# Four local edits to a four-sublayer encoder kernel: value products in banks of their own, another order of units in the down projections, the bias lines as rounded products, and turned blocks placed in two steps

## The chip, the cores and the metric

The kernel runs on one core of a Trainium2 chip. A core has a matrix engine (TensorE, PE in the profile, with its weight loads shown apart as PEld), a vector engine (VectorE, DVE), an engine for activations (ScalarE, ACT), one for general work (GpSimd, POOL) and one that here only issues transfers (SyncE, SP). PE writes into PSUM, eight banks of 128 partitions by 512 f32 numbers; everything else lies in SBUF or in device memory. The metric is the device time of one execution in microseconds.

## The reference

The input is 256 positions of 2048 numbers. Two layers run one after the other, each a token mixer and a gated MLP, all with a root-mean-square norm ahead and a residual sum behind:

```python
def reference(x, ...):
    h = x
    for i in range(2):
        hn = rms_norm(h, mix_norm[i])
        if i % 2 == 0:
            h = h + mixer_a(hn, ...)      # 16 query heads, 4 key heads, rotary positions, dense softmax
        else:
            h = h + mixer_b(hn, ...)      # 3 groups of 8 heads, dilations 1, 4, 16, windowed softmax
        h = h + conv_ffn(rms_norm(h, ffn_norm[i]), ...)
    return rms_norm(h, final_norm)

def conv_ffn(h, w_up, conv_w, conv_b, w_down):
    u = conv_width_3(h @ w_up, conv_w) + conv_b
    gate, val = split(u, 2)               # 5632 columns each
    return (silu(gate) * val) @ w_down

# in mixer_b, for each group g:
    bias = rel_bias_g[t5_bucket(rel * dilation)]          # 32 buckets x 8 heads
    logits = q k^T * scale + bias, -1e30 outside the window
    o = softmax(logits) @ v               # the value product
# and the groups are weighted by their softmax denominators
```

All of it is f32, and the weights (430 MB) pass through the core once.

## The kernel before

**Rounded halves.** The f32 products are made of three products of a rounded f32 type (F32R): a number is a high part, rounded by ACT, and a low part, which DVE gets by subtraction. A weight block is a `raw` of 512 KB (128 x 1024 numbers). `split_raw` turns it into `wh` (line 128, ACT) and `wl` (line 129, DVE), and `feed` makes 12 matmuls of 512 columns with it: high by high (line 153), low by high (154), high by low (155). Six `raw` buffers are loaded ahead by SP's queue. The split parts have a ring of three buffers, of four in the down projections.

**What sets the order.** The program is written as one long row of `feed` calls. Everything else (evacuation of a finished accumulator, rotary turn, softmax, convolution, residual sums) is a Python generator in the list `pending`, and `step()` runs the next piece of the first of them behind each half `feed`, so that its instructions stand between matmuls in the program. A scheduler then puts each engine's instructions in order by priority. `split_raw` gets 45 places of priority ahead of where it is written, so that splits pass other work on ACT and DVE. Within one engine the order is then fixed.

**PSUM.** Banks 0 to 3 hold the accumulators of projections, two at a time. Banks 4 to 7 are handed out in turn by `ps_tile()` for all that is small: transposes, scores, value products, bias lines.

**Value products (mixer B).** Group g has four heads in each half `hf` of the heads. `v_gen` runs by a plan, one entry a step: probabilities are scaled and turned (`turn`), put in place (`place`), rounded (`low`), multiplied (`value`). `value(i)` makes six matmuls of 256 columns for g = 0 (lines 307 to 309) into half a bank, then `split` reads it: `ah` on ACT (line 290), `al` on DVE (line 291). Heads 0 and 1 share a bank, and so do heads 2 and 3:

```python
                    def value(i):
                        j = i % 2
                        if j == 0:
                            parts["o"] = ps_tile()
```

**Down projections.** Two blocks of 512 output columns are made together in `project_pair`. Of the k-blocks, two (`SKG`) are multiplied by a scheme of seven products of sums in place of eight ("P" units of 6 matmuls; the products 1, 5, 6, 7 go into banks `M1`, `M5`, `M6`, `M7`, the others straight into an accumulator), and the others as usual ("c" units of 12 matmuls, into `C11`, `C21` or `C12`, `C22`). A P unit may need a sum of two raw blocks, which DVE makes (line 242). `weave` lays the units in a row. In the pair (0, 1) four c units stand first, then P and c units in turn until the c units run out; in the pair (2, 3) one stands first. When a block's last unit is done, its accumulator is added to the residual `h` by DVE (line 408). `combine` makes the sums of the seven products (lines 625 to 637). `late_at` is the first unit of the last k-block: before it, all pending work is drained.

**Bias lines (mixer B's bias, made during the first MLP).** `bias_lines` is a side generator that `step()` advances when fewer than two others are pending. It loads a one-hot table `oh` of 128 x 1024 (which bucket a distance falls in) and the 32 x 24 table of biases `rb`, spreads the biases over 32 columns each (`lh`, line 902, DVE) and makes `lh^T oh` in f32: six matmuls (line 908), two of 512 and four of 256 columns. DVE copies each out (`lnt`, line 911) and POOL's queue stores it to device memory (line 915), from where mixer B reads it much later.

**Turned blocks.** A transposition of 128 x 1024 numbers is made by DVE in 32 x 32 blocks (`turn_blocks`, line 335), and 16 copies put the blocks where they belong (`place_blocks`): 4 by POOL (line 345), 12 by ACT (line 347). `turned` issues all 16 in one step; `late_transpose` and `heads_T_dve` then wait two steps before they use the result.

Of the kernel before, what the change touches and what calls it, by code (L numbers as in the profile page):

```python
# [7 lines left out]
F32 = mybir.dt.float32  # L8
F32R = mybir.dt.float32r
AF = mybir.ActivationFunctionType  # L10
ALU = mybir.AluOpType
AX = mybir.AxisListType

P = 128
# [19 lines left out]
def tile_encoder(ctx: ExitStack, tc: tile.TileContext, x, xT, w_a, w_ao, q_gain, k_gain, w_b, w_bo,  # L34
                 rel_bias, gains, w_up, conv, w_down, final_norm, rope, ident_c, onehot, out):
    nc = tc.nc
# [23 lines left out]
    def nm(s):  # L60
        uid[0] += 1
        return f"{s}_{uid[0]}"
# [6 lines left out]
    def ps_tile():  # L69
        bank_at[1] = (bank_at[1] + 1) % 4  # L70
        return bank(4 + bank_at[1], "ps")
# [221 lines left out]
    def split_scaled(hi, lo, src, sc):  # L293
        nc.scalar.activation(hi, src, AF.Copy, scale=sc)
        if lo is None:
            return
        nc.vector.scalar_tensor_tensor(lo, src, sc, hi.bitcast(F32), ALU.mult, ALU.subtract)
# [18 lines left out]
    def new_hT(kt):  # L316
        t = hpool.tile([P, 2 * NT], F32R, tag=f"x{kt}", name=nm("xh"))
        return t[:, :NT], t[:, NT:], t
# [13 lines left out]
    def turn_blocks(s, pool, tag):  # L332
        t = pool.tile([P, 2, 512], F32, tag=tag, name=nm("tT"))
        for m in range(2):
            nc.vector.transpose(t[:, m], s[:, m])
        return t

    def place_blocks(o, t, place, part=range(16)):
        tv = t.rearrange("p m (j q c) -> p j m q c", j=4, q=4)
        for i in part:  # L340
            a, b = i // 4, (i // 4 + i) % 4
            dst = o[32 * b:32 * b + 32, :, :, 32 * a:32 * a + 32]
            src = tv[32 * a:32 * a + 32, :, :, b]
            if place[b] == "p":
                nc.gpsimd.tensor_copy(dst, src)  # L345
            elif place[b] == "a":
                nc.scalar.activation(dst, src, AF.Copy)  # L347
            else:
                nc.vector.tensor_copy(dst, src)

    def turned(o, s, pool, tag):
        t = turn_blocks(s, pool, tag)
        yield
        place_blocks(o.rearrange("p j (m t) -> p j m t", m=2), t, "paaa")

    def late_transpose(hT, n, g, pool, tags):
        def put(kt, src):
            hT[kt] = new_hT(kt)
            split_scaled(*hT[kt][:2], src, gain[:, g, kt:kt + 1])

        yield
        if n < 3:
            yield
            o = pool.tile([P, 4, NT], F32, tag=tags[1], name=nm("tM"))
            yield from turned(o, h[:, :, n * 512:(n + 1) * 512], pool, tags[0])
            yield
            yield
            for j in range(4):
                if j == 2:
                    yield  # L370
                put(4 * n + j, o[:, j, :])
            return
        yield
        for kp in range(2):
            if kp:
                yield
            t = ps_tile()
            for j in range(2):
                kt = 4 * n + 2 * kp + j
                for m in range(2):  # L380
                    nc.tensor.transpose(t[:, j * NT + m * P:j * NT + (m + 1) * P],
                                        h[:, m, kt * P:(kt + 1) * P], ident)
            for j in range(2):
                put(4 * n + 2 * kp + j, t[:, j * NT:(j + 1) * NT])
# [31 lines left out]
    def ffn(l, hT, ss_in, g_next, last, side=None):  # L416
        with tc.tile_pool(name=nm("wpool"), bufs=1) as wp, tc.tile_pool(name=nm("fpool"), bufs=1) as fp:
# [3 lines left out]
            part = small.tile([P, 2], F32, tag="part", name=nm("part"), bufs=1)  # L421
# [97 lines left out]
            for hf, (p0, p1) in enumerate(HALVES):  # L519
# [89 lines left out]
                ps = [("P", k, p) for k in SKG[hf] for p in ORDER]  # L609
                def weave(lead):  # L610
                    c, units = list(cs), []
                    units += [c.pop(0) for _ in range(lead)]
                    for u in ps:
                        units += [u] + [c.pop(0) for _ in range(min(1, len(c)))]
                    return units + c

                hl_ring.insert(0, (wp, 9))
# [90 lines left out]
    def heads_T_dve(o, s, pool, tag):  # L708
        hi, lo = o
        dst = hi if lo is None else s.rearrange("p m c -> p (m c)").rearrange("p (j t) -> p j t", j=4)  # L710
        yield from turned(dst, s, pool, tag)
        yield
        yield
        if lo is not None:
            split(hi, lo, dst)
# [175 lines left out]

    def bias_lines(wp, lp):
        if True:
            oh = wp.tile([P, 1024], F32, tag="wh9", name="oh")
            nc.gpsimd.dma_start(oh, onehot)
            rb = lp.tile([P, 32], F32, name="rb")[:, :24]
            nc.gpsimd.memset(rb, 0.0)
            nc.gpsimd.memset(rb[32:33, :], -1e30)
            nc.gpsimd.dma_start(rb[:32, :], rel_bias)
            lh = wp.tile([P, 24, 32], F32, tag="wl9", name="lh")  # L900
            lnt = lp.tile([P, 2, 512], F32, tag="tT", name="lnt")
            nc.vector.tensor_copy(lh, rb[:, :, None].to_broadcast([P, 24, 32]))
            for b in range(6):
                for _ in range(2):
                    yield
                c0, w = ((0, 512), (512, 256), (768, 256))[b // 2]
                t = ps_tile()
                nc.tensor.matmul(t[:, :w], lh[:, 4 * b:4 * b + 4, :].rearrange("p a r -> p (a r)"),
                                 oh[:, c0:c0 + w], start=True, stop=True)
                ln = lnt[:, b % 2]  # L910
                nc.vector.tensor_copy(ln[:, :w], t[:, :w])
                dst = scr0[4 * b:4 * b + 4] if b < 2 else scr1[4 * (b - 2):4 * (b - 2) + 4]
                for i in range(4):
                    yield
                    nc.gpsimd.dma_start(dst[:, 32 * i:32 * i + 32, :], ln[:, :w])

    def mixer_b(hT, ss_in):
        with tc.tile_pool(name="bpool", bufs=1) as bp:
# [26 lines left out]
            for hf in range(2):  # L945
# [56 lines left out]
                def v_gen(g, accs, hf=hf, probs=probs, e=e):  # L1002
# [31 lines left out]
                        split(*parts[i], src)  # L1034

                    def value(i):
                        j = i % 2
                        if j == 0:
                            parts["o"] = ps_tile()
                        o, pT = parts["o"], parts.pop(i)  # L1040
                        for kt in range(2):
                            vs = (allp, kt, slice(i * P, (i + 1) * P))
                            if g == 0:
                                mm3(o[:, j * NT:(j + 1) * NT], v, pT, vs,
                                    (allp, slice(kt * NT, (kt + 1) * NT)), kt == 0, kt == 1)
                            else:
                                mm3(o[:, j * NT + kt * P:j * NT + (kt + 1) * P], v, pT, vs,
                                    (allp, slice(kt * P, (kt + 1) * P)), True, True)
                        sl = (2 * g + hf) * 4 + i
                        slots[sl] = new_slot(sl)  # L1050
                        split(*slots[sl], o[:, j * NT:(j + 1) * NT])
# [110 lines left out]
```

## Time and profile before

| | |
|---|---|
| time, median of 3 runs | 2263.91 us (2262.77 to 2263.95) |
| the profiled execution | 2264.28 us, its span 2262.5 us |
| PE busy | 2241.2 us, 99% of the span |
| DVE busy | 1671.3 us, 74% |
| ACT busy | 1535.6 us, 68% |
| POOL busy | 299.2 us, 13% |
| matmuls of 512 columns in F32R | 9527, one every 0.227 us where nothing waits |
| moved | 437 MB, 193 GB/s over the span |

The profile page gives busy time of each engine, the span in 40 slices, the DMA queues, the chain of work that ended last, and groups of instructions by line. In a row of the timeline stand the start, the time taken, the engine, the line, the operation, what is written and read, the shape, and in brackets the idle time ahead with what ended it. Matmuls overlap in the pipeline, so the time of one in a row (0.39 us) is longer than the step from one start to the next (0.23 us); what is lost is read from the starts. The profiled execution is 0.37 us over the median of the runs, and 1.8 us of it lie outside its span.

### The profile page before, as it was taken

What the parts mean: (1) busy time and instruction counts of PE and PEld (TensorE: products, weight loads), DVE (VectorE), ACT (ScalarE), POOL (GpSimd) and SP (SyncE); (2) the same over time, 40 slices, a digit from 0 to 9 for tenths busy, and PEclk for the clock granted to TensorE, in tenths of its full rate; (3) what the DMA queues carried; (4) which work ended last, traced back from release to release, by engine and by line L of the source; (5) the groups of instructions that cost most, each with busy time, mean ns of one, the idle gap of its engine ahead of it and who ended that gap; (6) DMA issues with size and microseconds to landing.
All of it is one profiled execution on the core that took longest, in us unless ns stands there. A gap on an engine that the chain in (4) does not pass through costs nothing.

```text
span 2262.5 us, 28925 instructions
## 1 busy us (share of the span) xinstructions
PE 2241.2 (99%) x10093; PEld 1853.5 (82%) x10093; DVE 1671.3 (74%) x2267; ACT 1535.6 (68%) x2400; POOL 299.2 (13%) x436
## 2 busy tenths in 40 slices
PE   9999999999999999999999999999999999999998
PEld 7788888888888888888878887888888888888886
DVE  6776678888878788856575557465888788688895
ACT  6665777777547777767775777565777754577763
POOL 2211102210001010121130103000101100001101
PEclk9999999999999999999999999999999999999999
DMA  8444667765665655666655564655665656556654
GB/s 297 158 149 149 191 198 217 227 198 192 207 203 187 199 190 188 204 223 203 190 173 180 177 194 160 186 195 188 197 191 192 204 188 212 188 193 193 226 191 136
DMA packets 126452, 437.43 MB, mean 193 GB/s; under 512 B 17265, under 2 KB 18033, under 8 KB 126305
## 3 DMA queue, kind: packets, MB, share of 16 engines
q1 hardware_dynamic: 119744, 425.64, 58.3%
q0 software_dynamic: 6128, 9.38, 1.7%
q8 instruction: 79, 1.29, 0.2%
q14 instruction: 69, 0.56, 0.1%
q10 hardware_dynamic: 432, 0.56, 0.1%
HBM read 429.20 MB, written 6.29 MB: 192 GB/s over the span
## 4 chain that ended last, share of the span: by engine, by line
PE 91%; DVE 3%; ACT 2%; issue 1%; DMA 1%; POOL 1%; SPq 0%; POOLq 0%; DVEq 0%; ACTq 0%
PE acc L154 25%; PE acc L155 25%; PE acc L153 25%; PE acc L273 5%; PE acc L275 5%; PE acc L278 5%; DVE wl L129 1%; ACT tM L347 1%; ACT wh L128 1%; PE ps L305 1%; PE ps L307 0%; PE ps L309 0%; POOL pp L345 0%; PE ps L308 0%; DMA raw<-in_w_down_dram 0%
## 5 line engine op out<-in xcount | busy, mean ns | idle before, releaser
L129 DVE TENSOR_TENSOR wl<-raw,wh 128x1024 fp32r<-128x1024 f32 x828 | 1019.0, 1237 | 437.8 <-ACT wh L128 435.2
L128 ACT ACTIVATE wh<-raw 128x1024 fp32r<-128x1024 f32 x828 | 872.6, 1058 | 499.9 <-PE acc L155 307.0
L153 PE MATMUL acc<-wh,xh 128*128 128x512 f32 x2176 | 851.2, 392 | 0.6 <-ACT wh L164 0.6
L154 PE MATMUL acc<-wl,xh 128*128 128x512 f32 x2176 | 848.2, 390 | 1.6 <-DVE wl L129 1.4
L155 PE MATMUL acc<-wh,xh 128*128 128x512 f32 x2176 | 847.7, 390 | 0.0
L154 PEld LDWEIGHTS acc<-wl,xh 128*128 128x128 f32 x2176 | 408.8, 188 | 88.6 <-DVE wl L129 4.4
L155 PEld LDWEIGHTS acc<-wh,xh 128*128 128x128 f32 x2176 | 408.6, 188 | 84.7
L153 PEld LDWEIGHTS acc<-wh,xh 128*128 128x128 f32 x2176 | 408.9, 188 | 84.0 <-ACT wh L164 1.0
L345 POOL COPY u<-t 32x256 f32<-32x256 f32 x176 | 110.6, 628 | 1027.1 <-DVE t L455 1018.9
L273 PE MATMUL acc<-wh,ah 128*128 128x512 f32 x520 | 202.5, 389 | 1.5 <-DVE h L408 1.5
L275 PE MATMUL acc<-wh,al 128*128 128x512 f32 x520 | 202.3, 389 | 0.0
L154 PE MATMUL acc<-wl,ah 128*128 128x512 f32 x480 | 187.1, 390 | 1.0 <-DVE wl L129 1.0
L153 PE MATMUL acc<-wh,ah 128*128 128x512 f32 x480 | 187.2, 390 | 0.3 <-DVE cu L628 0.3
L155 PE MATMUL acc<-wh,al 128*128 128x512 f32 x480 | 186.8, 390 | 0.0
L347 ACT ACTIVATE u<-t 32x256 f32<-32x256 f32 x352 | 147.7, 420 | 13.9 <-DVE t L455 6.0
L278 PE MATMUL acc<-wl,ah 128*128 128x512 f32 x520 | 146.1, 389 | 0.0
L273 PEld LDWEIGHTS acc<-wh,ah 128*128 128x128 f32 x520 | 97.6, 188 | 22.6 <-DVE h L408 2.3
L278 PEld LDWEIGHTS acc<-wl,ah 128*128 128x128 f32 x520 | 97.6, 188 | 20.3
L275 PEld LDWEIGHTS acc<-wh,al 128*128 128x128 f32 x520 | 97.6, 188 | 20.2
L154 PEld LDWEIGHTS acc<-wl,ah 128*128 128x128 f32 x480 | 90.2, 188 | 20.0 <-DVE wl L129 1.8
L153 PEld LDWEIGHTS acc<-wh,ah 128*128 128x128 f32 x480 | 90.1, 188 | 19.1 <-DVE cu L628 0.9
L155 PEld LDWEIGHTS acc<-wh,al 128*128 128x128 f32 x480 | 90.1, 188 | 18.6
(182 smaller groups left out, 1729.0 us busy)
## 6 DMA issues: line engine op xcount, KB each, us to landing
raw<-in_w_up_dram SPq DMA_DIRECT2D x352, 512.0 KB, 4.4
raw<-in_w_down_dram SPq DMA_DIRECT2D x176, 512.0 KB, 4.8
raw<-in_w_b_dram SPq DMA_DIRECT2D x144, 512.0 KB, 4.4
raw<-in_w_bo_dram SPq DMA_DIRECT2D x48, 512.0 KB, 3.9
raw<-in_w_a_dram SPq DMA_DIRECT2D x40, 512.0 KB, 4.5
raw<-in_w_ao_dram SPq DMA_DIRECT2D x32, 512.0 KB, 4.0
raw<-in_w_a_dram SPq DMA_DIRECT2D x16, 256.0 KB, 6.6
h<-in_x_dram SPq DMA_DIRECT2D x4, 512.0 KB, 8.4
```

Source lines behind the costliest of these rows:

```text
L128: nc.scalar.activation(wh, r, AF.Copy)
L129: nc.vector.tensor_tensor(wl, r, wh.bitcast(F32), ALU.subtract)
L153: nc.tensor.matmul(accs[m], xh, wh[:, j, :], start=st, stop=False)
L154: nc.tensor.matmul(accs[m], xh, wl[:, j, :], start=False, stop=False)
L155: nc.tensor.matmul(accs[m], xl, wh[:, j, :], start=False, stop=sp)
L273: nc.tensor.matmul(acc[k], xh, wh[:, j, :], start=k in fresh, stop=False)
L275: nc.tensor.matmul(acc[k], xl, wh[:, j, :], start=False, stop=False)
L278: nc.tensor.matmul(acc[k], xh, wl[:, j, :], start=False, stop=last[k] == i and j == 1)
L305: nc.tensor.matmul(o, lh[ls], rh[rs], start=start, stop=stop)
L345: nc.gpsimd.tensor_copy(dst, src)
L347: nc.scalar.activation(dst, src, AF.Copy)
```

## The change

Four things change.

1. `value`: for the first group (g = 0) each of the four value products takes a bank of its own, and uses its first half. For the other groups nothing changes.
2. `weave`: in the pair (0, 1) of the first half of either MLP, no c unit follows the first P unit of each k-block. The two c units that are left over stand at the end: the row ends P7, c, P6, c, P4, c in place of P7, c, P6, P4. P4's product goes into `C21`, the last c unit's into `C12` and `C22`. `late_at` moves from unit 21 to unit 23.
3. `bias_lines`: the one-hot rows 0 to 63 are loaded twice, into partitions 0 to 63 and 64 to 127, and rounded by ACT (line 907 of the new kernel); the biases are loaded twice as well, `rs` holds their high parts in the upper rows and, by a subtraction, the low parts in the lower (lines 908, 909), and `lh` is spread from it in F32R (910). One F32R matmul then sums both parts. Two more steps stand between the loads and the use.
4. `turned`: eight copies are issued in one step and eight in the next. The users wait one step less in exchange, so that they come in the same step as before.

```diff
     def turned(o, s, pool, tag):
         t = turn_blocks(s, pool, tag)
-        yield
-        place_blocks(o.rearrange("p j (m t) -> p j m t", m=2), t, "paaa")
+        for part in (range(8), range(8, 16)):
+            yield
+            place_blocks(o.rearrange("p j (m t) -> p j m t", m=2), t, "paaa", part)
...
             yield from turned(o, h[:, :, n * 512:(n + 1) * 512], pool, tags[0])
             yield
-            yield
...
                     units += [c.pop(0) for _ in range(lead)]
+                    lone = (ps[0], ps[7]) if lead > 1 and hf == 0 else ()
                     for u in ps:
-                        units += [u] + [c.pop(0) for _ in range(min(1, len(c)))]
+                        units += [u] + [c.pop(0) for _ in range(min(1, len(c))) if u not in lone]
                     return units + c
...
         yield from turned(dst, s, pool, tag)
         yield
-        yield
...
-            oh = wp.tile([P, 1024], F32, tag="wh9", name="oh")
-            nc.gpsimd.dma_start(oh, onehot)
+            of = lp.tile([P, 2, 512], F32, tag="tT", name="of").rearrange("p a c -> p (a c)")
+            oh = wp.tile([P, 1024], F32R, tag="wh9", name="oh")
             rb = lp.tile([P, 32], F32, name="rb")[:, :24]
+            rs = lp.tile([P, 32], F32R, name="rs")[:, :24]
             nc.gpsimd.memset(rb, 0.0)
             nc.gpsimd.memset(rb[32:33, :], -1e30)
-            nc.gpsimd.dma_start(rb[:32, :], rel_bias)
-            lh = wp.tile([P, 24, 32], F32, tag="wl9", name="lh")
+            for i in range(2):
+                nc.gpsimd.dma_start(of[64 * i:64 * i + 64], onehot[:64])
+                nc.gpsimd.dma_start(rb[64 * i:64 * i + 32, :], rel_bias)
+            yield
+            yield
+            lh = wp.tile([P, 24, 32], F32R, tag="wl9", name="lh")
             lnt = lp.tile([P, 2, 512], F32, tag="tT", name="lnt")
-            nc.vector.tensor_copy(lh, rb[:, :, None].to_broadcast([P, 24, 32]))
+            nc.scalar.activation(oh, of, AF.Copy)
+            nc.vector.tensor_copy(rs, rb)
+            nc.vector.tensor_tensor(rs[64:], rb[64:], rs[64:].bitcast(F32), ALU.subtract)
+            nc.vector.tensor_copy(lh, rs.bitcast(F32)[:, :, None].to_broadcast([P, 24, 32]))
...
                     def value(i):
-                        j = i % 2
+                        j = 0 if g == 0 else i % 2
```

On DVE, where the first half's value products of group 0 are split, the order before is this (`al` and `pTl` are low parts, `tp` turned probabilities of the next group, `ps_1991` the bank of heads 0 and 1):

```order
L129 TENSOR_TENSOR wl_2013_10468<-raw_2004_10433,wh_2012_10467 128x1024
L291 TENSOR_TENSOR al_1993_10394<-ps_1991_10386,ah_1992_10393 128x256
L291 TENSOR_TENSOR pTl_1997_10414<-pp_1980_10325,pTh_1996_10413 128x512
L1017 STREAM_TRANSPOSE tp_2020_10513<-pr_1893_9829 128x2x128
L1013 TENSOR_SCALAR pr_1940_10114<-pr_1940_10114,e_1707_8857 128x128 x2
L1013 TENSOR_SCALAR pr_1947_10143<-pr_1947_10143,e_1707_8857 128x128
L1017 STREAM_TRANSPOSE tp_2058_10705<-pr_1940_10114 128x2x128
L129 TENSOR_TENSOR wl_2019_10498<-raw_2016_10493,wh_2018_10497 128x1024
L291 TENSOR_TENSOR al_1999_10424<-ps_1991_10386,ah_1998_10423 128x256
```

and after the change the same stretch of DVE reads:

```order
L129 TENSOR_TENSOR wl_2014_10476<-raw_2005_10441,wh_2013_10475 128x1024
L291 TENSOR_TENSOR al_1993_10401<-ps_1991_10393,ah_1992_10400 128x256
L291 TENSOR_TENSOR pTl_1997_10421<-pp_1980_10332,pTh_1996_10420 128x512
L1025 STREAM_TRANSPOSE tp_2022_10522<-pr_1893_9836 128x2x128
L1021 TENSOR_SCALAR pr_1940_10121<-pr_1940_10121,e_1707_8864 128x128 x2
L1021 TENSOR_SCALAR pr_1947_10150<-pr_1947_10150,e_1707_8864 128x128
L1025 STREAM_TRANSPOSE tp_2060_10714<-pr_1940_10121 128x2x128
L129 TENSOR_TENSOR wl_2021_10507<-raw_2018_10502,wh_2020_10506 128x1024
L291 TENSOR_TENSOR al_2000_10432<-ps_1998_10424,ah_1999_10431 128x256
```

No row has moved; head 1 is read from `ps_1998`, a bank other than head 0's `ps_1991`, where before both rows read `ps_1991`.

On DVE at the start of the first MLP, where the bias tables are waited for, stands before (`xh` are the low parts of the normed input, `ps` a transposed block of `h`):

```order
L297 SCALAR_TENSOR_TENSOR xh_2684<-ps_2679,gain,xh_2684 128x256
L902 COPY lh<-rb 128x768
L297 SCALAR_TENSOR_TENSOR xh_2687<-ps_2679,gain,xh_2687 128x256
L129 TENSOR_TENSOR wl_2758<-raw_2738,wh_2757 128x1024
L297 SCALAR_TENSOR_TENSOR xh_2715<-ps_2710,gain,xh_2715 128x256
L297 SCALAR_TENSOR_TENSOR xh_2718<-ps_2710,gain,xh_2718 128x256
L129 TENSOR_TENSOR wl_2778<-raw_2773,wh_2777 128x1024
```

and after:

```order
L297 SCALAR_TENSOR_TENSOR xh_2684<-ps_2679,gain,xh_2684 128x256
L297 SCALAR_TENSOR_TENSOR xh_2687<-ps_2679,gain,xh_2687 128x256
L908 CAST rs<-rb 128x24
L129 TENSOR_TENSOR wl_2758<-raw_2738,wh_2757 128x1024
L297 SCALAR_TENSOR_TENSOR xh_2715<-ps_2710,gain,xh_2715 128x256
L909 TENSOR_TENSOR rs<-rb,rs 64x24
L910 CAST lh<-rs 128x768
L297 SCALAR_TENSOR_TENSOR xh_2718<-ps_2710,gain,xh_2718 128x256
L129 TENSOR_TENSOR wl_2778<-raw_2773,wh_2777 128x1024
```

The row that waits for the loads of `rb` is now the cast `rs`, one row further on and right ahead of `wl_2758`; the subtraction and the spread stand behind `wl_2758`. On ACT the rounding of `oh` (line 907) comes in between `xh_2715` and `xh_2718`. On POOL's queue the loads are four in place of two, in the order `of`, `rb`, `of`, `rb`.

On DVE at the join of the two pairs in the first half of the first MLP (`acc_983` to `acc_986` are `C11`, `C21`, `C12`, `C22` of the pair (0, 1); `wl_1093` and later belong to the pair (2, 3)) stands before:

```order
L408 TENSOR_TENSOR h_82<-acc_985_5005,h_82 128x512
L129 TENSOR_TENSOR wl_1087_5546<-raw_1085_5543,wh_1086_5545 128x1024
L408 TENSOR_TENSOR h_82<-acc_986_5006,h_82 128x512
L129 TENSOR_TENSOR wl_1090_5558<-raw_1088_5555,wh_1089_5557 128x1024
L408 TENSOR_TENSOR h_82<-acc_984_5004,h_82 128x512
L129 TENSOR_TENSOR wl_1093_5576<-raw_1091_5573,wh_1092_5575 128x1024
```

and after:

```order
L129 TENSOR_TENSOR wl_1087_5553<-raw_1085_5550,wh_1086_5552 128x1024
L408 TENSOR_TENSOR h_82<-acc_984_5011,h_82 128x512
L129 TENSOR_TENSOR wl_1090_5565<-raw_1088_5562,wh_1089_5564 128x1024
L633 TENSOR_TENSOR h_82<-h_82,cu_1070_5492 128x512
L242 TENSOR_TENSOR raw_1085_5550<-raw_1085_5550,raw_1095_5594 128x1024
L129 TENSOR_TENSOR wl_1093_5583<-raw_1091_5580,wh_1092_5582 128x1024
L408 TENSOR_TENSOR h_82<-acc_985_5012,h_82 128x512
L408 TENSOR_TENSOR h_82<-acc_986_5013,h_82 128x512
```

The residual sum of `acc_984` stood last of the three before, and stands ahead of the others now, one split earlier.

## The prediction, made blind

> **What bounds the kernel now.** I read the busy times first, then the chain of work that ended last, then what PE waits for.
>
> ```profile
> PE 2241.2 (99%) x10093; PEld 1853.5 (82%) x10093; DVE 1671.3 (74%) x2267; ACT 1535.6 (68%) x2400; POOL 299.2 (13%) x436
> PE 91%; DVE 3%; ACT 2%; issue 1%; DMA 1%; POOL 1%; SPq 0%; POOLq 0%; DVEq 0%; ACTq 0%
> ```
>
> PE carries the kernel, and no edit takes a 512-column matmul of the weight stream away. So the change can only win what PE loses between matmuls, or what small matmuls cost too much; and it can lose wherever it delays a split that PE needs. PE's own waits, longest first:
>
> ```profile
> PE ps L307 <- DVE al L291: 4.5, 2, 2.3
> PE acc L154 <- DVE wl L129: 2.4, 5, 0.7
> PE acc L273 <- DVE h L408: 1.5, 2, 1.0
> ```
>
> The columns are total, times, longest. The first and the third row are the places of edits 1 and 2. The bias matmuls of edit 3 are work, not waits, and stand in the timeline. That is little in 2262.5 us: this is a case of small sums.
>
> **Edit 1, value products.** PE at the first half's heads 0 and 1, and DVE beside it:
>
> ```profile
> 1162.77 0.28 PE L307 MATMUL ps<-pTh,vh 128*128 128x256 f32 x1
> 1163.48 0.40 PE L153 MATMUL acc<-wh,xh 128*128 128x512 f32 x1
> 1165.76 0.39 PE L154 MATMUL acc<-wl,xh 128*128 128x512 f32 x1
> 1165.99 0.39 PE L155 MATMUL acc<-wh,xh 128*128 128x512 f32 x1
> 1168.63 0.39 PE L307 MATMUL ps<-pTh,vh 128*128 128x256 f32 x1 [2.26 <-DVE al L291]
> 1175.43 0.39 PE L155 MATMUL acc<-wh,xh 128*128 128x512 f32 x1
> 1175.87 0.39 PE L307 MATMUL ps<-pTh,vh 128*128 128x256 f32 x1
> ```
> ```profile
> 1167.02 1.22 DVE L129 TENSOR_TENSOR wl<-raw,wh 128x1024 fp32r<-128x1024 f32 x1
> 1168.16 0.42 DVE L291 TENSOR_TENSOR al<-ps,ah 128x256 fp32r<-128x256 f32 x1
> 1181.24 1.23 DVE L129 TENSOR_TENSOR wl<-raw,wh 128x1024 fp32r<-128x1024 f32 x1 [2.38 <-ACT wh L128]
> ```
>
> Head 0 was multiplied at 1162.77. Its low part `al` runs on DVE only at 1168.16, behind scalings and a split, and head 1, in the same bank, must wait for it. Starts are 0.23 apart where nothing waits (1165.76, 1165.99), so the stall costs 1168.63 − 1165.99 − 0.23 = 2.41 us. With a bank of its own, head 1 has nothing to wait for there. Heads 2 and 3 have the same wait at 1175.87, of 1175.87 − 1175.43 − 0.23 = 0.21. The row of waits counts two such places of about equal length (4.5 in 2), one for each half, so 2 × 2.6 = 5.2 us are there to be had.
>
> What is late next? DVE is nearly full in this stretch:
>
> ```profile
> 1162.70:1176.70 14.00, 11.69 (x63) 9.51 (x62) 13.55 (x31) 11.23 (x21) 7.50 (x11) 1.00 0.48 152
> 1185.11 0.39 PE L154 MATMUL acc<-wl,xh 128*128 128x512 f32 x1
> ```
>
> DVE is busy 13.55 of 14.00 us. If PE comes 2.6 earlier, DVE does not. But the splits were made ahead: the tightest I found behind the stall is the one that ends at 1181.24 + 1.23 = 1182.47 and is used at 1185.11, a slack of 2.64 us, which is just what is needed. I take the full 2.6 for each half, so −5.2, with bounds −3.5 (a third lost to that split and its successors) and −5.6 (PE's earlier progress also frees buffers earlier).
>
> **Edit 3, bias lines.** A 512-column and a 256-column bias matmul, each with its neighbours:
>
> ```profile
> 363.74 1.02 PE L908 MATMUL ps<-oh,lh 128*128 128x512 f32 x2
> 364.83 0.40 PE L154 MATMUL acc<-wl,xh 128*128 128x512 f32 x1
> 398.19 0.59 PE L908 MATMUL ps<-oh,lh 128*128 128x256 f32 x2
> 398.86 0.40 PE L154 MATMUL acc<-wl,xh 128*128 128x512 f32 x1
> ```
>
> Between the start of the bias matmul and that of line 154 one matmul of line 153 lies as well. So the f32 form costs 364.83 − 363.74 − 0.23 = 0.86 us at 512 columns and 398.86 − 398.19 − 0.23 = 0.44 at 256. The rounded form costs 0.23 at 512, and 0.12 at 256 as the value products show (six in 1163.48 − 1162.77 = 0.71). Saved: 2 × 0.63 + 4 × 0.32 = 2.5 us, all on PE's path.
>
> Against it stands the start of the side work:
>
> ```profile
> 274.13 0.54 POOL L899 DMA_DIRECT2D rb<-in_rel_bias_dram  x1
> 279.31 0.56 DVE L902 COPY lh<-rb 128x768 f32<-128x768 f32 x1 [4.06 <-DMA rb<-in_rel_bias_dram]
> 280.18 1.22 DVE L129 TENSOR_TENSOR wl<-raw,wh 128x1024 fp32r<-128x1024 f32 x1
> 281.67 0.40 PE L154 MATMUL acc<-wl,xh 128*128 128x512 f32 x1
> 283.28 3.50 DVE L129 TENSOR_TENSOR wl<-raw,wh 128x1024 fp32r<-128x1024 f32 x3 [0.46 <-ACT wh L128]
> oh<-in_onehot_dram POOLq DMA_DIRECT2D x1, 512.0 KB, 5.7
> rb<-in_rel_bias_dram POOLq DMA_DIRECT2D x1, 3.0 KB, 5.1
> ```
>
> DVE stands still for 4.06 us until `rb` has landed, and everything behind it on DVE waits too. The split at 280.18 ends at 281.40 and PE uses it at 281.67: 0.27 us of slack, no more. After the change `rs` waits for the second `rb`, the fourth load in the queue in place of the second. Two more issues of about 0.55 each put its issue near 275.3, and with the 5.1 us of the row it lands near 280.4; if the bytes set the time (the same 512 KB, begun at about 273.5, 5.7 us) near 279.2. Behind it DVE now has only the small cast ahead of the split (the spread of 0.56 went behind it, and one `xh` of 0.48 ahead), so the split ends about 1.5 us after landing: at 280.7 to 281.9, against the 281.67 of its use. The next split (283.28) waited for its `wh`; it now has the subtraction and the spread ahead of it, some 0.8 us, and on ACT the rounding of `oh` ahead of the `xh` and `wh` it needs. I take +0.3 us, between 0 (early landing) and +1.2 (late landing and the spread in full).
>
> The Trainium skill, "DMA: Bandwidth & Descriptors", section "Anatomy of one DMA — SWDGE (gpsimd) path", gives about 2 us plus the bytes at 436 GB/s for one such transfer, by which 512 KB would land after 3.2 us and this term would be 0. The trace has 5.7 us for it, so I do not rest on that.
>
> The bias matmuls come two steps later, and POOL's stores of them with them. `u` copies of the convolution stand between them on POOL. POOL is busy 13% of the span, and the stores are read only in mixer B; what hides them is that idle time, and if it were gone one row of four stores, 2.74 us of issue, would stand ahead of a convolution's copies. Cost taken: nothing.
>
> **Edit 2, the order of units.** PE and DVE at the join of the pairs, first MLP and second:
>
> ```profile
> 596.85 0.61 PE L278 MATMUL acc<-wl,ah 128*128 128x512 f32 x2
> 597.24 0.69 DVE L408 TENSOR_TENSOR h<-acc,h 128x512 f32<-128x512 f32 x1
> 597.98 0.50 PE L273 MATMUL acc<-wh,ah 128*128 128x512 f32 x1 [0.52 <-DVE h L408]
> 1865.86 0.61 PE L278 MATMUL acc<-wl,ah 128*128 128x512 f32 x2
> 1867.45 0.50 PE L273 MATMUL acc<-wh,ah 128*128 128x512 f32 x1 [0.98 <-DVE h L408]
> ```
>
> P4 is last, writes `C21`, and the next pair's first unit needs that bank, so PE waits for the residual sum. Two matmuls take 2 × 0.23 of each stretch: 597.98 − 596.85 − 0.46 = 0.67, and 1867.45 − 1865.86 − 0.46 = 1.13, in all 1.8 us. After the change a c unit of 12 × 0.23 = 2.7 us into other banks lies between. In the new order one split (1.23) and one sum (0.69) stand on DVE between the end of P4 and the moment `C21` is free, so 1.9 of 2.7. The wait goes: −1.8, or −1.1 if the larger one alone goes.
>
> The price is that the first two P units of a k-block follow each other with no c between, twice in a pair: two units of 1.4 us in a row. These two need no sum on DVE, so DVE and ACT owe 2 × 1.23 and 2 × 1.06 in 2.7 us.
>
> ```profile
> 535.00:597.00 62.00, 62.00 (x275) 51.36 (x274) 53.26 (x61) 38.24 (x48) 2.58 (x4) 1.00 0.56 182
> raw<-in_w_down_dram SPq DMA_DIRECT2D x176, 512.0 KB, 4.8
> ```
>
> Over this stretch of the first MLP PE never stands still, with DVE busy for 53.26 of 62.00. The splits run ahead of PE there by a ring of four. I take 0, with bounds 0 and +1.0 in all.
>
> **Edit 4, turned blocks.** At mixer A's keys:
>
> ```profile
> 69.71 0.84 ACT L347 ACTIVATE ro<-tT 32x256 f32<-32x256 f32 x2
> 70.64 1.06 ACT L290 ACTIVATE kTh<-ro 128x1024 fp32r<-128x1024 f32 x1
> 71.00 0.50 PE L154 MATMUL acc<-wl,xh 128*128 128x512 f32 x1 [0.49 <-DVE wl L129]
> 74.15 0.50 PE L154 MATMUL acc<-wl,xh 128*128 128x512 f32 x1
> ```
>
> In the new order a split on ACT passes two of the copies (0.84 us), so the wait at 71.00 goes. But the copies still stand ahead of `kTh` and of the next split, which do not move, so the same lateness shows at 74.15, two splits on. Net 0, between −0.9 and +0.3. Elsewhere the rows hardly move: this edit does next to nothing.
>
> **The sum.** −5.2 − 2.5 + 0.3 − 1.8 + 0 = −9.2. From the profiled execution's 2264.28 us that is 2255.1. This execution stood 0.37 over the median of 2263.91, so by the median 2254.7; I say 2255.0. The terms' bounds add to −4.6 at one end (−3.5 − 2.5 + 1.2 − 1.1 + 1.0 + 0.3) and −10.8 at the other (−5.6 − 2.5 + 0 − 1.8 − 0.9), so 2259.7 to 2253.5.
>
> **Rivals.** (a) The gain of edit 1 is eaten by DVE behind it. For: 13.55 of 14.00 us busy, and a slack that is just met. Against: the wait row names `al` alone. If all but 0.5 of each half's 2.6 were given back, the sum is −9.2 + 4.2 = −5.0: 2259.
>
> (b) The bias loads land late. For: a store on the same queue landed after 12.1 us:
>
> ```profile
> scr<-lnt POOLq DMA_DIRECT2D x8, 256.0 KB, 12.1
> ```
>
> Then `rs` holds DVE 12.1 − 5.1 = 7.0 us longer, and PE behind it: −9.2 + 7.0 = −2.2, so 2262, no difference that can be told. Against: that is a store, and the loads of before took 5.1 and 5.7.
>
> (c) Slower: the lone P units bring the need of raw blocks forward, and a load is no longer ahead. It would show as PE waiting at four places (two in a pair, two MLPs), up to a whole load of 4.8 us each: −9.2 + 19.2 = +10, so 2274. It decides from (9.2 + 4.5)/4 = 3.4 us a place. For: blocks of two units in a row are asked for 2.7 us sooner. Against: PE lost nothing in 62 us there, with the queue at 0.56 of the DMA engines' time.
>
> (d) Slower too: PE's clock falls where the banks now change with each product. The window above shows 1.00 with banks handed out in turn already. Half the clock over both such stretches would cost 2 × 11.69 = 23.4: 2264.28 − 9.2 + 23.4 = 2278. The Trainium skill, "TensorE: Matmul & The Clock Gate", section "A second HAM failure mode: psum-queue depth-cycling", tells of such an oscillation of the clock when a kernel cycles through banks; the trace does not bear it out so far.
>
> **Chances.** The forecast 0.73, (a) 0.12, (b) 0.06, (c) 0.07, (d) 0.02. What a measurement here can tell from no change is about 0.2%, 4.5 us. Forecast and nearly all of (a), at the edge of it, are faster: 0.84. The same: (b) and 0.01 each of (a) and (c), 0.08. Slower: the rest of (c) and (d), 0.08. The range takes the terms' bounds and most of (a): 2252.5 to 2260.5.
>
> **What would show it.** Right: no row `PE ps L307 <- DVE al` among PE's waits, none of `PE acc L273 <- DVE h L408` at the first join; bias matmuls starting 0.23 and 0.12 before their successors; PE going on past 281.67 with at most 0.3 us lost. Wrong: new PE waits on `wl` just after the value products (a), DVE waiting on `rb` past 281 (b), PE or DVE waiting on a raw load in the first pair of a down projection (c), a clock under 1.00 in the value stretch (d).

## The result, and the profile after

| | before | changed |
|---|---|---|
| median of 6 runs | 2263.93 us (2262.23 to 2266.0) | 2254.59 us (2253.57 to 2256.46) |
| ratio to before, 95% interval | | 0.9961 (0.995 to 0.9973) |
| the profiled execution, and its span | 2264.28, 2262.5 | 2253.57, 2251.8 |

The change makes the kernel 9.3 us faster; 2255.0 was forecast. The page of the changed kernel, its busy times and the chain that ended last:

```profile
PE 2235.8 (99%) x10087; PEld 1852.7 (82%) x10087; DVE 1670.6 (74%) x2269; ACT 1536.3 (68%) x2401; POOL 302.1 (13%) x438
PE 94%; issue 2%; DVE 1%; ACT 1%; DMA 1%; POOL 1%; SPq 0%; POOLq 0%; DVEq 0%; ACTq 0%
```

PE has 94% of the chain in place of 91%. Its waits (total, times, longest):

```profile
PE acc L154 <- DVE wl L129: 3.9, 5, 1.6
PE ps L396 <- DVE warm L393: 1.5, 1, 1.5
PE ps L309 <- DVE qTl L291: 0.6, 1, 0.6
PE acc L154 <- DVE wl L165: 0.2, 1, 0.2
```

The wait on `al` (4.5) and the one on `h` (1.5) are gone, and the wait on `wl` has grown from 2.4 to 3.9, with a longest of 1.6 that was not there.

**Value products.** PE at the second head of the first half, in the timeline, DVE's read of the first head's bank, and the window that answers to the one shown of before (the first head starts at 1159.58 here):

```profile
1162.84 0.39 PE L155 MATMUL acc<-wh,xh 128*128 128x512 f32 x1
1163.06 0.28 PE L307 MATMUL ps<-pTh,vh 128*128 128x256 f32 x1
```
```profile
1164.96 0.42 DVE L291 TENSOR_TENSOR al<-ps,ah 128x256 fp32r<-128x256 f32 x1
```
```profile
1159.50:1173.50 14.00, 14.00 (x75) 11.97 (x74) 13.77 (x32) 12.66 (x24) 7.51 (x11) 1.00 0.49 153
```

Head 1 starts 0.22 after the matmul ahead of it, where it was 2.64. VectorE reads head 0 as late as before, 1164.96 − 1159.58 = 5.4 us after its first matmul (1168.16 − 1162.77 then), but PE is already past head 1. PE does not stand still in the whole stretch.

**The start of the first MLP.** PE, and beside it DVE:

```profile
280.16 0.39 PE L153 MATMUL acc<-wh,xh 128*128 128x512 f32 x1
282.15 0.50 PE L154 MATMUL acc<-wl,xh 128*128 128x512 f32 x1 [1.60 <-DVE wl L129]
```
```profile
280.77 0.18 DVE L908 CAST rs<-rb 128x24 fp32r<-128x24 f32 x1 [5.78 <-DMA rb<-in_rel_bias_dram]
280.87 1.23 DVE L129 TENSOR_TENSOR wl<-raw,wh 128x1024 fp32r<-128x1024 f32 x1
```

Here is the new wait: DVE stands 5.78 us on the biases, the split behind the cast comes late, and PE loses 282.15 − 280.16 − 0.23 = 1.76 us, and 0.2 more one unit later.

**The bias matmuls** in the groups of the page (count, busy, mean ns of one): 

```profile
L916 PE MATMUL ps<-oh,lh 128*128 128x256 f32 x4 | 1.1, 278 | 0.0
L916 PE MATMUL ps<-oh,lh 128*128 128x512 f32 x2 | 0.8, 389 | 0.0
```

Six instructions in place of twelve, each as long as any rounded matmul of its width (0.28 and 0.39 in the rows of the value products and of the weight stream).

**The join of the pairs.** In the first MLP the last unit, a c, starts its low parts at 593.03, and the next pair starts without a gap:

```profile
593.03 1.07 PE L278 MATMUL acc<-wl,ah 128*128 128x512 f32 x4
593.94 0.39 PE L273 MATMUL acc<-wh,ah 128*128 128x512 f32 x1
```
```profile
591.58 0.68 DVE L408 TENSOR_TENSOR h<-acc,h 128x512 f32<-128x512 f32 x1
```

The sum of `C21` ends at 592.26, 1.7 us before its bank is written again.

### The profile page after: what moved, and what is told of

It is laid out like the page before. It is cut to its first block, busy times and chain, and to the rows that moved or that the text cites. A ratio compares the mean times of both kernels' runs of the same rounds, so it can differ in the third digit from the quotient of the medians.

```text
span 2251.8 us, 28923 instructions
## 1 busy us (share of the span) xinstructions
PE 2235.8 (99%) x10087; PEld 1852.7 (82%) x10087; DVE 1670.6 (74%) x2269; ACT 1536.3 (68%) x2401; POOL 302.1 (13%) x438
## 4 chain that ended last, share of the span: by engine, by line
PE 94%; issue 2%; DVE 1%; ACT 1%; DMA 1%; POOL 1%; SPq 0%; POOLq 0%; DVEq 0%; ACTq 0%
PE acc L154 25%; PE acc L155 25%; PE acc L153 25%; PE acc L278 5%; PE acc L273 5%; PE acc L275 5%; DVE wl L129 1%; PE ps L305 1%; PE ps L309 1%; PE ps L308 1%; PE ps L307 0%; PE ps L868 0%; ACT tM L347 0%; ACT wh L128 0%; DMA xt<-in_xT_dram 0%
```

## The experiments

Twelve kernels were run. For those with one edit alone or one undone, the table puts side by side what PE lost at six places in one profile of each: the distance between two starts, less the usual one. "Values" is all four places of both halves, "loads" the two splits behind the bias loads, "joins" the first and the second MLP, "keys" mixer A's two places together, "955" a place that the prediction did not speak of.

| kernel | median us | ratio to before (95%) | values | loads | joins | keys | 955 |
|---|---|---|---|---|---|---|---|
| before | 2263.93 | | 5.3 | 0 | 0.7, 1.1 | 0.95 | 0.65 |
| changed | 2254.59 | 0.9961 (0.995 to 0.9973) | 0 | 2.0 | 0, 0 | 1.04 | 0 |
| edit 1 alone | 2256.68 | 0.9972 (0.9962 to 0.9982) | 0 | 0.3 | 0.4, 0 | 0.96 | 0.66 |
| edit 2 alone | 2262.23 | 0.9994 (0.9985 to 1.0003) | 5.0 | 0.2 | 0, 0 | 0.92 | 0.65 |
| edit 3 alone | 2263.36 | 0.9998 (0.9989 to 1.0007) | 5.2 | 2.2 | 0, 0.6 | 0.90 | 0.64 |
| edit 4 alone | 2262.53 | 0.9994 (0.9985 to 1.0003) | 5.2 | 0 | 0, 0 | 1.05 | 0 |
| changed, edit 2 undone | 2255.41 | 0.9964 (0.995 to 0.9978) | 0 | 2.3 | 1.2, 1.3 | 1.04 | 0 |
| changed, edit 4 undone | 2254.48 | 0.9962 (0.9949 to 0.9974) | 0 | 1.2 | 0, 0 | 0.95 | 0.64 |

The times of single edits of a microsecond or two cannot be told from no change; the places can. A profile is one execution, and some places differ from one to the next, so that is read with the other profiles in view.

**Edit 1 alone.** The kernel before with

```diff
-                        j = i % 2
+                        j = 0 if g == 0 else i % 2
```

> Only edit 1: the four value products of the first group take a bank each. If the terms are local and add, as the sum had it: 5.2 us less than before, no PE wait on al, and PE's starts at the second and fourth head back to back. If VectorE behind it is the bound (rival a): 1 to 3 us less, with new PE waits on wl within some 20 us behind the value products.

It took 2256.68 us, 7.2 less than the kernel before in the same session (2263.86). The wait on `al` is no longer among PE's waits, and the one on `wl` is what it was:

```profile
PE acc L154 <- DVE wl L129: 2.4, 5, 0.8
```

So nothing was given back behind the value products, and rival (a) falls. The interval, 4.1 to 8.6 us, holds the 5.3 that the places show.

**Heads further apart.** The kernel before, with no bank more:

```diff
-                        j = i % 2
+                        j, k = (i // 2, i % 2) if g == 0 else (i % 2, 0)
                         if j == 0:
-                            parts["o"] = ps_tile()
-                        o, pT = parts["o"], parts.pop(i)
+                            parts["o", -1 - k] = ps_tile()
+                        o, pT = parts["o", -1 - k], parts.pop(i)
```

> The kernel before, but heads 0 and 2 share a bank of the first group, and 1 and 3, in place of 0 and 1, 2 and 3; no bank more than before. If the wait comes from reading a bank back too soon after it was written: the wait on al goes as with four banks, 5 us less, since two steps lie between. If the number of banks matters (a bank in turn still busy): the wait stays, or half of it.

2256.70 us, ratio 0.9973 (0.9963 to 0.9983), the same as with four banks, and no wait on `al`. So it is not the number of banks: what cost the time was writing a bank again one step after it was filled, while the read of it stood behind other work on VectorE. The two heads lie in different halves of the bank, and PE waited all the same; why the whole bank is waited for, no run tried.

**Edit 2 alone**, the order of units with `lone` in `weave`:

```diff
+                    lone = (ps[0], ps[7]) if lead > 1 and hf == 0 else ()
-                        units += [u] + [c.pop(0) for _ in range(min(1, len(c)))]
+                        units += [u] + [c.pop(0) for _ in range(min(1, len(c))) if u not in lone]
```

> Only edit 2: the order of units in the first pair. Local terms: 1.8 us less, no PE wait on h at the join of the pairs. If the lone P units need raw blocks too early (rival c): PE waits on raw loads or on wl in the first pair of either MLP, and no gain or a loss of up to 10 us.

**Edit 2 undone** in the changed kernel:

```diff
-                    lone = (ps[0], ps[7]) if lead > 1 and hf == 0 else ()
+                    lone = ()
```

> The changed kernel with edit 2 undone. If edit 2 is worth the 1.8 us of the one profile: 1.8 us more than the changed kernel, with a PE wait on h at both joins. If the wait at the joins hangs on how late the raw loads happen to come, as the other runs with the old order show (0 to 1.2 us at one join): some 0.7 us more, a wait at one join or none.

Alone it took 2262.23 us, and PE shows no wait on `h`. Undone, the time is 2255.41, and PE waits at both joins:

```profile
PE acc L273 <- DVE h L408: 2.1, 2, 1.1
```

But in the profile of edit 4 alone, with the old order as well, there is no wait at either join. Six profiles have the old order (before, edits 1, 3 and 4 alone, heads further apart, edit 2 undone); the first join cost 0.7, 0.4, 0, 0, 1.2, 1.2 us in them and the second 1.1, 0, 0.6, 0, 0, 1.3, a mean of 1.1 us for both together. What goes along with it is how long DVE stood some 25 us earlier in front of a sum of raw blocks. The row with the longest wait ahead of the first join, edit 2 undone and then edit 4 alone:

```profile
571.04 1.23 DVE L242 TENSOR_TENSOR raw<-raw,raw 128x1024 f32<-128x1024 f32 x1 [3.91 <-DMA raw<-in_w_down_dram]
```
```profile
570.13 1.23 DVE L242 TENSOR_TENSOR raw<-raw,raw 128x1024 f32<-128x1024 f32 x1 [3.21 <-DMA raw<-in_w_down_dram]
```

Over the twelve joins, the five with such a wait of 3.9 us or more (there are five: 4.34, 3.91, 4.20, 4.05, 4.04) lost 0.7 to 1.3 us; of the seven with 3.42 or less, five lost nothing, and the others 0.4 and 0.6. It may be that DVE carries the lateness of a load down to the join. That goes with the numbers; no run held the loads' time fixed, so it is not shown beyond that. With the new order no join was late in any of the eight profiles that have it.

**More lone units.** The changed kernel, with three lone P units in each k-block in place of one:

```diff
-                    lone = (ps[0], ps[7]) if lead > 1 and hf == 0 else ()
+                    lone = ps[0:3] + ps[7:10] if lead > 1 and hf == 0 else ()
```

> The changed kernel, but three P units of each k-block stand alone in place of one, so that four P units follow one another, one of them with a sum. If the splits have slack there, as the prediction took it: at most 0.5 us lost at each of the four places, 0 to 2 us more than the changed kernel. If raw blocks are needed too early (rival c): 1 to 4.8 us at each place, 4 to 19 us more, with waits on raw loads.

2255.03 us, ratio 0.9965 (0.9953 to 0.9978); the changed kernel has 0.9961. In the pairs that are pressed PE loses 0.3 us at one place of the first MLP and 0.2 at one of the second, behind VectorE:

```profile
PE acc L278 <- DVE wl L129: 0.2, 1, 0.2
```

PE has no other wait in either pair. Three times the pressure costs next to nothing, and rival (c) falls.

**Edit 3 alone**, `bias_lines` as in the change, with nothing else (`...` marks what is left out here and in the diffs below):

```diff
...
+            for i in range(2):
+                nc.gpsimd.dma_start(of[64 * i:64 * i + 64], onehot[:64])
+                nc.gpsimd.dma_start(rb[64 * i:64 * i + 32, :], rel_bias)
+            yield
+            yield
...
+            nc.scalar.activation(oh, of, AF.Copy)
+            nc.vector.tensor_copy(rs, rb)
...
```

> Only edit 3: the bias lines as rounded products. If the late loads alone make the wait that the changed kernel shows at the first MLP's start: 2.5 us won on the six matmuls, 2.0 us lost there, so 0.5 less, with a PE wait on wl of 1.6 us. If the wait there needs the other edits: 2.5 us less and no such wait.

2263.36 us, 0.5 less than before, as the local terms had it, though by its interval from 2.5 less to 1.6 more fits too. The wait at the MLP's start is there without the other edits:

```profile
280.59 0.39 PE L153 MATMUL acc<-wh,xh 128*128 128x512 f32 x1
282.81 0.50 PE L154 MATMUL acc<-wl,xh 128*128 128x512 f32 x1 [1.84 <-DVE wl L129]
```

**The use of the loads put off.** The changed kernel; the loads stay where they are, and what reads them also reads a column made from the convolution's taps (times 0, plus 1), so that the scheduler cannot put it earlier:

```diff
...
+            one = lp.tile([P, 8], F32, name="one")[:, :1]
+            nc.vector.tensor_scalar(one, cw[:, :1], 0.0, 1.0, op0=ALU.mult, op1=ALU.add)
-            nc.scalar.activation(oh, of, AF.Copy)
-            nc.vector.tensor_copy(rs, rb)
+            nc.scalar.activation(oh, of, AF.Copy, scale=one)
+            nc.vector.scalar_tensor_tensor(rs, rb, one, rb, ALU.mult, ALU.max)
```

> The changed kernel, but the cast of the biases and the rounding of the one-hot table also read a column that the convolution's taps give, so that both engines reach them some 17 us later, when the loads have long landed; the loads themselves stay. If the wait on the loads, standing ahead of the splits, makes the 1.8 and 0.2 us lost at 280 and 285: these go, about 2 us less than the changed kernel, 2252.6, and no PE wait on wl there. If PE is late there for another reason (the order of xh and wh rows): the wait stays.

2252.28 us (2252.16 to 2252.79), ratio 0.9954 (0.994 to 0.9968). PE loses nothing at 280 and 285, and the long wait on `wl` is gone from its waits:

```profile
PE acc L154 <- DVE wl L129: 2.3, 4, 0.9
```

That is the cause shown by taking it away: the loads themselves cost nothing, only that the instructions which wait for them stand ahead of splits without slack.

**The biases first in the queue.** The changed kernel, with

```diff
             for i in range(2):
-                nc.gpsimd.dma_start(of[64 * i:64 * i + 64], onehot[:64])
                 nc.gpsimd.dma_start(rb[64 * i:64 * i + 32, :], rel_bias)
+            for i in range(2):
+                nc.gpsimd.dma_start(of[64 * i:64 * i + 64], onehot[:64])
```

> The changed kernel with both loads of the biases written ahead of the loads of the one-hot table; on the queue one 256 KB load then still stands ahead of them and one behind. If each 256 KB ahead in the queue costs the small load time to land: it lands about 1.2 us earlier than the 6.9 us after issue of the changed kernel, below 6 us. If the small load takes its 6.9 us by itself: no change.

One run, 2253.32 us. The rows of `rb` (least, middle and most of the times to landing) here and in the changed kernel:

```profile
DMA to landing us min/median/max: 4.5/4.7/4.8
```
```profile
DMA to landing us min/median/max: 5.9/6.4/6.9
```

With one 256 KB transfer ahead of the biases in place of two, the loads of 3 KB land 4.8 and 4.5 us after their issue, where the second took 6.9; PE loses 0.3 us. What stands ahead in the queue can explain that, but one execution does not show it: in the changed kernel the first load of the biases, with one such transfer ahead as well, took 5.9. The spread from one execution to the next is as large: the same order of loads as in the changed kernel landed its last `rb` after 7.1, 5.5, 7.2 and 6.0 us in four other profiles (edit 3 alone, more lone units, edit 2 undone, edit 4 undone), and PE lost 2.2, 0.7, 2.3 and 1.2 us there, one for one with the landing. The order of before, with one 512 KB transfer ahead, landed its one load of 3 KB after 4.5 to 5.3 us in five profiles (before, edits 1, 2 and 4 alone, heads further apart), so the new order is the slower one.

**The biases at the kernel's start.** The changed kernel, with

```diff
     nc.gpsimd.dma_start(ident, ident_c)
+    rb = cpool.tile([P, 32], F32, name="rb")[:, :24]
+    nc.gpsimd.memset(rb, 0.0)
+    nc.gpsimd.memset(rb[32:33, :], -1e30)
+    for i in range(2):
+        nc.gpsimd.dma_start(rb[64 * i:64 * i + 32, :], rel_bias)
...
```

> The changed kernel with the biases loaded at the kernel's start; the one-hot table is loaded where it was. VectorE then has nothing to wait for, but the order puts ScalarE's rounding of the table ahead of the split that PE needs at 280.4. If any wait on those loads that stands ahead of a split costs the same: a PE wait there of 1 to 2 us, now behind ScalarE. If VectorE's place alone matters: no wait.

One run, 2254.65 us. With no table ahead of them, the two loads of 3 KB land 4.9 and 4.8 us after their issue, no sooner than in the run before. DVE no longer waits at the first MLP, but the order put ACT's rounding of the one-hot table ahead of the split:

```profile
280.10 1.06 ACT L908 ACTIVATE oh<-of 128x1024 fp32r<-128x1024 f32 x1 [5.03 <-DMA of<-in_onehot_dram]
281.07 1.04 ACT L133 ACTIVATE wh<-raw 128x1024 fp32r<-128x1024 f32 x1
```
```profile
282.16 0.50 PE L158 MATMUL acc<-wh,xh 128*128 128x512 f32 x1 [1.22 <-ACT wh L133]
283.42 0.51 PE L159 MATMUL acc<-wl,xh 128*128 128x512 f32 x1 [0.76 <-DVE wl L134]
```

PE loses 1.4 and 1.0 us (280.55 is the start ahead of the first), no less than the 2.0 of the changed kernel. The wait has only changed its engine.

**Edit 4 alone**, `turned` in two steps:

```diff
-        yield
-        place_blocks(o.rearrange("p j (m t) -> p j m t", m=2), t, "paaa")
+        for part in (range(8), range(8, 16)):
+            yield
+            place_blocks(o.rearrange("p j (m t) -> p j m t", m=2), t, "paaa", part)
...
-            yield
...
-        yield
```

> Only edit 4: turned blocks placed in two steps. Local terms: no change, within 0.3 us; at mixer A's keys the wait on wl at 71.0 goes, the one at 74.15 grows by as much. Rival: the two waits go together, 0.9 us less; or the later copies delay their users, and it is slower.

**Edit 4 undone** in the changed kernel, the same lines the other way round.

> The changed kernel with edit 4 undone. If edit 4 wins what the profile of it alone shows: the PE wait on wl of 0.65 us some 955 us into the kernel is back, and the two at mixer A's keys (0.65 and 0.3) stand in place of one of 1.04; 0.6 us more in all. If it does nothing, as the prediction took it: no wait at 955.

At mixer A's keys 0.95 us became 1.05, all of it in one place: no gain, as forecast. But at 955, late in the first MLP, edit 4 wins 0.65 us. PE and ACT before:

```profile
956.71 0.50 PE L154 MATMUL acc<-wl,ah 128*128 128x512 f32 x1 [0.49 <-DVE wl L129]
```
```profile
949.20 5.11 ACT L347 ACTIVATE tM<-tT 32x256 f32<-32x256 f32 x12
954.33 2.01 ACT L128 ACTIVATE wh<-raw 128x1024 fp32r<-128x1024 f32 x2
```

and ACT with edit 4 alone:

```profile
948.65 2.55 ACT L347 ACTIVATE tM<-tT 32x256 f32<-32x256 f32 x6
951.22 1.06 ACT L128 ACTIVATE wh<-raw 128x1024 fp32r<-128x1024 f32 x1
952.31 1.27 ACT L347 ACTIVATE tM<-tT 32x256 f32<-32x256 f32 x3
953.60 1.06 ACT L128 ACTIVATE wh<-raw 128x1024 fp32r<-128x1024 f32 x1
```

Three more of the twelve copies stand ahead of these rows, so the order is nine copies, a split, three copies, a split. Twelve copies in a row held two splits for 5.1 us; in two steps a split comes in between, and PE does not wait. With edit 4 undone the loss of 0.64 is back. In the time this does not show: 2254.48 with it undone, 2254.59 with it, and alone 2262.53 with a ratio that takes in 1.

**Both mended.** The changed kernel with the late use of the loads, and at mixer A's keys, where DVE stood still, four of ACT's twelve copies given to DVE:

```diff
...
-                yield from heads_T_dve(kT, ro, ap, "sq")
+                yield from heads_T_dve(kT, ro, ap, "sq", PLACE)
...
```

(`PLACE` is "pava"; `heads_T_dve` and `turned` pass it on to `place_blocks`.)

> The changed kernel with two things mended: the late use of the bias loads of the run before, and at mixer A's keys four of the twelve ScalarE copies given to VectorE, which stood idle there for 2.35 us. If ScalarE's row of copies makes the 1.04 us lost at 71.7: it goes, and with the 2 us at 280 the time is about 3 us under the changed kernel, 2251.5. If VectorE's copies hold its own splits as long: the wait stays, 2252.5.

2251.61 us (2250.78 to 2252.99), ratio to before 0.9946 (0.9933 to 0.996), the fastest of all here. No loss is left at the keys, none at 280:

```profile
PE acc L154 <- DVE wl L129: 1.4, 3, 0.7
```

Against the late use alone, 2252.28, the times do not tell the two apart; the row of waits does, 1.4 for 2.3.

## Why the prediction was right, and where it was not

The forecast 2255.0 came out at 2254.59. That the two are only 0.4 apart is partly luck: two of the terms were wrong, one each way, two more were somewhat off, and the measured gain is known only to lie between 6.1 and 11.3 us (the interval of the ratio).

- **Edit 1, −5.2: right**, in size and in mechanism. Places: 5.3 to 0, and the matmul behind each of the four stalls is no longer 0.1 late either, so some 5.6 in all. What was feared next, the split with a slack of 2.64, did not become late: counted from the first head, PE came to it 2.8 us earlier (1179.11 − 1159.58 for 1185.11 − 1162.77), but the split ended 1.4 us earlier too, and 1.2 of slack is left (1176.50 + 1.42 in the row below). DVE was as full as before in the stretch (13.77 of 14.00), while ACT was busy for 12.66 where it had been for 11.23: it makes the high parts earlier when PE no longer stands still. That ACT gave the time is read from these windows, not tried.

```profile
1176.50 1.42 DVE L129 TENSOR_TENSOR wl<-raw,wh 128x1024 fp32r<-128x1024 f32 x1 [1.77 <-ACT wh L128]
```

- **Edit 3, −2.5: right** for the six matmuls.
- **Edit 3, +0.3 for the loads: wrong size.** The mechanism was as described (the cast ahead of a split with no slack), but the step "with the 5.1 us of the row it lands near 280.4" took the landing of a small load behind one transfer for that of a small load behind two of 256 KB and another small one. It measured 6.9 us here and 5.5 to 7.2 in four other profiles, so the term is 0.7 to 2.3 us, 1.7 in the mean of the five, and above the bound of 1.2 in three of them. The nearest row was not near: what stood ahead of it in the queue was different. How much of the 1.8 us between 5.1 and 6.9 is the queue's order and how much that one execution stays open. Rival (b) was this mechanism with a price of 7.0; the truth lay between.
- **Edit 2, −1.8: right for the execution that was read, too large as a mean.** The wait at the joins goes each time, but the old order loses 0 to 2.4 us there from one execution to another, 1.1 in the mean of six.
- **Edit 4, 0: wrong, by −0.65 us**, at the step "elsewhere the rows hardly move". They move at one place, at 955, where PE's row of waits on `wl` (2.4 in 5) had an entry there that the prediction gave no price. At the keys the forecast held.
- The rest: between the two profiles the terms give 5.3 + 2.5 + 1.8 − 2.0 − 0.1 + 0.65 = 8.2 us, and their spans differ by 10.7. About 1.2 of what is left lies in the first 55 us, which no edit touches (a wait of 0.34 on the same matmul stands at 54.99 before and at 53.81 after), and 0.4 is the late matmul behind each of the value stalls; the remainder lies in places that lose 0.5 us or less each and differ from one execution to the next.

Rivals (a) and (c) were put to the test and fell. Rival (d), a lower clock where each product has its bank: the value stretch of the changed kernel has a clock of 1.00, so not there; but see the last section.

## What to carry to other kernels

A PSUM bank that is shared by two products in a row turns the read of the first into a wait of the second; two banks used in turn do as well as four. An instruction that waits for a transfer costs nothing by itself, but everything that the order puts behind it on its engine waits too: put the use behind work that has slack, and do not price a transfer by one row of one execution in which other transfers stood ahead of it. And read a wait that hangs on transfers from more than one profile before its full size goes into a sum.

## What the runs showed of the hardware

A PE stall can cost more than itself, since the clock may fall behind it. With edit 3 alone, PE stood from 280.6 to 282.8, and the matmuls that follow start 0.43 us apart in place of 0.23, from 283.4 to 286.8; in the windows (PE's busy time stands behind the length, the granted clock behind POOL's):

```profile
280.00:282.60 2.60, 0.97 (x5) 0.47 (x3) 1.17 (x2) 1.06 (x1) 0.00 (x0) 1.00 0.07 24
282.60:287.60 5.00, 4.79 (x14) 3.81 (x15) 4.05 (x7) 2.69 (x4) 0.00 (x0) 0.66 0.45 130
287.60:292.60 5.00, 5.00 (x24) 4.12 (x23) 2.45 (x2) 1.79 (x2) 0.00 (x0) 1.00 0.79 261
```

A clock of 0.66 over 5 us is some 1.6 us lost on top of the 2.0 of the stall. The same happened with edit 2 alone, behind the first value stall (0.66 from 1167 to 1172), where the stall had been 2.4. It did not happen behind the stall of 2.4 in the second half of the same run, nor behind either of the two in before: of eleven stalls of 1.8 to 2.4 us in six profiles (before, edits 2, 3 and 4 alone, the changed kernel, edit 2 undone), two were followed by it. So a stall of this length is worth more on average than its own row says (an estimate: two times 1.6 us over eleven stalls, 0.3 us each), and the sum of edit 1 a little more than its places show.

Which stalls are followed goes with where they fall. In every one of the fourteen profiles the granted clock changes only at times that lie a whole number of steps of 3.413 us apart. Cut by these steps, edit 2 alone around its first value stall, and the kernel before around the same stall, are:

```profile
1164.82:1168.23 3.41, 1.18 (x8) 1.00 (x8) 3.41 (x10) 1.39 (x2) 0.00 (x0) 1.00 0.62 216
1168.24:1171.64 3.40, 3.40 (x9) 2.63 (x9) 3.40 (x9) 3.31 (x8) 3.19 (x5) 0.50 0.52 143
```
```profile
1164.75:1168.16 3.41, 1.62 (x8) 1.01 (x6) 3.20 (x8) 2.87 (x5) 0.00 (x0) 1.00 0.65 217
1168.17:1171.57 3.40, 2.94 (x16) 2.56 (x17) 3.40 (x9) 1.87 (x5) 1.80 (x3) 1.00 0.70 212
```

The two stalls that were followed lie whole in one step, with 2.4 and 2.0 us lost in it; the other nine lose at most 2.0 in any one step, as eight of them are cut by a border. The least of the two and the most of the nine are equal, so no limit can be read from these runs. The Trainium skill, "TensorE: Matmul & The Clock Gate", section "What's actually happening", tells of a gate that looks at windows of about 3.4 us which do not start with the kernel, and halves the clock after an idle one. The 3.4 us from 283.4 to 286.8 agree, and so does that it strikes some stalls and not others; that idle time of 2 us is enough, where the section speaks of an idle window, is what these runs add.
